# Chains of RWKV-7 in six phases that lanes go through in step, and TensorE's program in emission order

## The chip, the cores and the metric

The kernel runs on one core of one Trainium2 chip. The metric is the time of one execution on the device in microseconds (us); less is better. TensorE is written PE here, VectorE DVE, ScalarE ACT, GpSimd POOL and SyncE SP (it issues DMAs), as in the profile.

## The reference, cut to what matters

One layer of a diffusion backbone on 128 context tokens and 1024 latent tokens of 1024 channels, in float32. The hidden vector is projected once; half of the columns feed RWKV-7 (8 heads of 64, in two directions), half feed RG-LRU; both outputs are joined, projected and added to x under a gate; a gated feed-forward layer with a convolution follows. The change concerns the recurrence of RWKV-7 and what is computed beside it:

```python
def _wkv7_step(S, inp):
    r_t, w_t, kk_t, b_t, k_t, v_t = inp
    sa = jnp.einsum('dbhij,dbhj->dbhi', S, kk_t)
    S = S * w_t[..., None, :] - sa[..., :, None] * b_t[..., None, :] + v_t[..., :, None] * k_t[..., None, :]
    y = jnp.einsum('dbhij,dbhj->dbhi', S, r_t)
    return S, y

def block(x, cvec, s0, h0, grid, lp):
    mod = (jax.nn.silu(cvec) @ lp['w_mod'] + lp['b_mod'])[..., None, :]
    sh1, sc1, g1, sh2, sc2, g2 = jnp.split(mod, 6, axis=-1)
    h = rmsnorm(x, lp['ln1_g']) * (1.0 + sc1) + sh1
    proj = h @ lp['w_in']
    r, k, v, xw, xa, xg, xb, gb = jnp.split(proj, SPLITS, axis=-1)
    ya, s_fin = rwkv7_mix(r, k, v, xw, xa, xg, s0, ...)
    yb, h_fin = rglru_mix(xb, gb, h0, ...)
    x = x + g1 * (jnp.concatenate([ya, yb], axis=-1) @ lp['w_out'])
    h = rmsnorm(x, lp['ln2_g']) * (1.0 + sc2) + sh2
    u = dwconv(h @ lp['w_up'], lp['ffn_conv_w'], lp['ffn_conv_b'], CONV_F_LEFT, grid)
    ua, ub = jnp.split(u, 2, axis=-1)
    x = x + g2 * ((jax.nn.gelu(ua) * ub) @ lp['w_down'])
    return x, s_fin, h_fin
```

## The kernel before

The recurrence is computed in chunks of 64 tokens in each direction, two heads at a time. One visit to a chunk (both directions of a pair of heads) is a **hop**. A **lane** is a chain of hops that depend on each other through the state `S`; `chain` writes it as a Python generator. The program has two stretches of chains. In the first (437 to 737 us of the profiled execution) lanes a and b make 24 and 16 hops, beside the rest of the input projection and the RG-LRU branch (`rest_of_projection`: products `mm`, gate products `lg`, and long elementwise work and scans on DVE, ACT and POOL). In the second (737 to 960 us) lanes a, b, c and d make 8 hops each, beside the rest of the modulation (`mod_rest`, products `md` with `w_mod`, whose four quarters of the rows go to four column groups of the array), the RG-LRU half of the output projection (`wout_lru`, products `wo`) and `post` (the normalisation and gate of what the lanes leave, `po` on PE). The output projection's second half, and then the feed-forward layer (two thirds of the span), follow and are not touched.

On PE a hop is a row of small groups, each a few passes into one PSUM bank, which another engine empties. The names are the tiles' (the lane's letter last):

- `ya <- S, KR`: key and receptance rows times the state. Then `ya <- VS, G`, first halves; ACT and DVE (in the second stretch ACT alone, `use[1] = A`) copy the result to `R`.
- `ca <- R, TTp`: the inverse times `R`; copied to `VS` by the same engines.
- `ca <- VS, Kt`: the state's update, which DVE adds to `S`; then `ya <- VS, G`, second halves, copied to `o`.
- `prep` for the next hop, one step early: `pa <- kxa, BK` (DVE masks it into `G`; POOL scales `BK`), and `pa <- ident, BK` (transposes, which ACT copies to `Kt`). `fetch_keys` loads `BK` and, for a pair's second chunk, has ACT write the head blocks `kx`.

`chain` yields after the `R` copies, after the `VS` copies and at the hop's end. `run_all` takes a step from each generator in turn, in proportion to its count of steps, and so writes the program; a scheduler then orders each engine's instructions anew, by its own model of the times. Instructions of an engine run in that order on the chip. `deal` gives out the eight PSUM banks by name. In the first stretch each name of a lane has a bank of its own:

```python
deal(mm=(0, 1), lg=(0, 1), pa=(2,), ya=(3,), ca=(4,), yb=(5,), cb=(6,), pb=(7,))
```

and in the second all of `pa` to `pd`, `ca` to `cd` and `po` take banks 2 and 4 by turns, each name with a count of its own:

```python
two = (2, 4)
deal(ya=(3,), yb=(5,), yc=(0,), yd=(1,), pa=two, pb=two, pc=two, pd=two, ca=two[::-1], cb=two[::-1], cc=two[::-1],
     cd=two[::-1], md=(6,), wo=(7,), po=two)
run_all((lane_a, 98 - LA), (lane_b, 98 - LB), (lane_c, 26), (lane_d, 26), (posts(90), 90),
        (seq(mod_rest(16, 24), beside_all((mod_rest(24, 48), 30), (wout_lru(), 48))), FL))
```

The functions that the change touches, with the line numbers of the profile:

## Time and profile before

| | |
|---|---|
| median of 3 runs | 1852.57 us (1850.71 to 1853.16) |
| the profiled execution: time, span | 1849.17 us, 1847.5 us |
| PE busy, of the span | 1716.4 us, 93% |
| DVE, ACT, POOL busy | 69%, 47%, 39% |
| first stretch of chains | 437 to 737 us |
| second stretch of chains | 737 to 960 us |

Busy is the time in which an engine had an instruction under way; passes of PE overlap, so a group's end is not the next one's start. "Idle before" is the time an engine stood just ahead of an instruction, with what released it. The granted clock is the mean of TensorE's clock in a stretch, as a share of full speed (1.00 is 2.4 GHz, and 0.50 would be 1.2 GHz throughout).

### The profile page before, as it was taken

The numbers are of one execution on the slowest core, as the hardware profiler recorded it, in microseconds if no ns is written. First come the engines' busy times: TensorE is split into PE (matmuls) and PEld (weight loads), VectorE is DVE, ScalarE is ACT, GpSimd is POOL, SyncE is SP. The second block draws the span as 40 slices with busy tenths as digits, with TensorE's granted clock in tenths as the row PEclk, the third lists the DMA queues.
The fourth block names the chain that finished last, engine by engine and source line by source line (L and its number), as shares of the span: only waits on it lengthen the run. The fifth ranks groups of instructions, "written<-read, shape, count | busy, mean of one in ns | idle before, by whom it ended". The sixth has DMA issues, their size and how long they took to land.

```text
span 1847.5 us, 35759 instructions
## 1 busy us (share of the span) xinstructions
PE 1716.4 (93%) x13341; PEld 1442.9 (78%) x13341; DVE 1272.2 (69%) x2633; ACT 865.5 (47%) x1787; POOL 721.8 (39%) x742
## 2 busy tenths in 40 slices
PE   5998898888999989899988789999999998999996
PEld 4776676678777778456656689999999998888885
DVE  5458967797477664476788877676767667576764
ACT  6466655643666756333335844444444443121211
POOL 1022423322355344131121166666666663434340
PEclk8898979889999999899999899999999999999998
DMA  9254544443443434867775222222222225558571
GB/s 300 63 163 155 174 139 135 147 147 118 145 122 97 131 104 146 257 194 231 232 254 189 82 64 86 78 72 72 74 79 75 77 73 171 184 159 262 173 252 57
DMA packets 268428, 264.92 MB, mean 143 GB/s; under 512 B 21173, under 2 KB 218448, under 8 KB 268256
## 3 DMA queue, kind: packets, MB, share of 16 engines
q1 hardware_dynamic: 252496, 245.97, 42.1%
q10 hardware_dynamic: 15472, 16.54, 2.7%
q8 instruction: 105, 1.72, 0.4%
q14 instruction: 67, 0.55, 0.1%
q0 software_dynamic: 288, 0.14, 0.0%
HBM read 188.00 MB, written 74.58 MB: 142 GB/s over the span
## 4 chain that ended last, share of the span: by engine, by line
PE 66%; DVE 9%; ACT 3%; DMA 3%; issue 3%; POOL 3%; SPq 0%; ACTq 0%; POOLq 0%; DVEq 0%
PE acc L92 14%; PE x L92 7%; PE y L92 7%; PE z L92 7%; PE mm L92 7%; PE v L92 3%; PE wo L92 3%; PE ya L92 2%; PE lg L92 2%; PE md L92 2%; PE pa L92 2%; PE ca L92 1%; DVE X L501 1%; PE yb L92 1%; DVE gt L499 1%
## 5 line engine op out<-in xcount | busy, mean ns | idle before, releaser
L92 PE MATMUL mm<-h_hi,winp 128*128 128x384 f32 x1056 | 304.4, 358 | 4.9 <-DVE vr L808 3.2
L92 PEld LDWEIGHTS mm<-h_hi,winp 128*128 128x128 f32 x1056 | 198.7, 196 | 26.4 <-issue 14.9
L92 PE MATMUL mm<-h_lo,winp 128*128 128x384 f32 x528 | 187.7, 356 | 3.0 <-DVE h_lo L112 3.0
L112 POOL TENSOR_TENSOR wl<-raw,wh 128x512 fp32r<-128x512 f32 x110 | 155.1, 1412 | 69.7 <-ACT wh L106 69.4
L106 ACT ACTIVATE wh<-raw 128x512 fp32r<-128x512 f32 x110 | 69.5, 633 | 148.3 <-PE z L92 81.0
L92 PE MATMUL x<-f_hi,wh 128*128 128x256 f32 (+1 forms) x352 | 105.8, 301 | 8.9 <-ACT q L1652 5.3
L92 PEld LDWEIGHTS mm<-h_lo,winp 128*128 128x128 f32 x528 | 103.7, 197 | 9.6 <-DVE h_lo L112 4.5
L1090 POOL TENSOR_TENSOR BK<-BK,pc 128x256 f32<-128x256 f32 x72 | 47.8, 664 | 150.5 <-PE pa L92 58.8
L92 PE MATMUL x<-f_lo,wh 128*128 128x256 f32 (+1 forms) x352 | 105.5, 300 | 0.2 <-DVE f_lo L112 0.2
L92 PE MATMUL y<-t_hi,wh 128*128 128x320 f32 (+1 forms) x352 | 104.9, 298 | 0.7 <-DVE q L1657 0.7
L92 PE MATMUL x<-f_hi,wl 128*128 128x256 f32 (+1 forms) x352 | 105.3, 299 | 0.0
L92 PE MATMUL y<-t_lo,wh 128*128 128x320 f32 (+1 forms) x352 | 104.7, 297 | 0.0
L92 PE MATMUL y<-t_hi,wl 128*128 128x320 f32 (+1 forms) x352 | 104.6, 297 | 0.0
L112 POOL TENSOR_TENSOR wl<-S,wh 128x512 fp32r<-128x512 f32 x44 | 57.7, 1311 | 105.6 <-ACT wh L106 105.6
L92 PE MATMUL acc<-f_hi 128*128 128x512 f32 x330 | 91.0, 397 | 3.2 <-ACT zf L1760 3.2
L108 POOL TENSOR_SCALAR t_hi<-raw 128x512 fp32r<-128x512 f32 x66 | 52.9, 804 | 81.6 <-PE acc L92 35.4
L1619 DVE SCALAR_TENSOR_TENSOR zf<-C,fcw,zf 128x567 f32<-128x567 f32 x66 | 63.5, 962 | 23.3 <-ACT zf L1617 23.3
L92 PEld LDWEIGHTS acc<-f_hi 128*128 128x128 f32 x330 | 63.1, 192 | 16.9 <-ACT zf L1760 3.7
L92 PEld LDWEIGHTS x<-f_hi,wh 128*128 128x128 f32 x352 | 67.9, 193 | 9.9 <-ACT q L1652 5.8
L112 DVE TENSOR_TENSOR t_hi<-raw,t_hi 128x512 fp32r<-128x512 f32 x66 | 48.1, 735 | 37.0 <-POOL t_hi L108 37.0
L1617 ACT ACTIVATE zf<-C,colB,fcw 128x576 f32<-128x576 f32 x66 | 57.3, 868 | 28.1 <-DVE C L1689 15.7
L600 POOL TENSOR_TENSOR kd<-kd,rk 128x512 f32<-128x512 f32 (+1 forms) x24 | 32.2, 1342 | 97.0 <-ACT kd L598 96.8
(516 smaller groups left out, 5211.1 us busy)
## 6 DMA issues: line engine op xcount, KB each, us to landing
raw<-in_w_down SPq DMA_DIRECT2D x132, 256.0 KB, 3.1
raw<-in_w_up SPq DMA_DIRECT2D x88, 256.0 KB, 3.0
wmod<-in_w_mod SPq DMA_DIRECT2D x68, 256.0 KB, 4.2
act_d<-zf SPq DMA_DIRECT2D x44, 288.0 KB, 2.2
src<-act_d SPq DMA_DIRECT2D x66, 192.0 KB, 3.8
win<-in_w_in SPq DMA_DIRECT2D x44, 256.0 KB, 3.9
KR<-kb_d SPq DMA_DIRECT2D x36, 256.0 KB, 3.2
VS<-v_d SPq DMA_DIRECT2D x36, 256.0 KB, 3.2
```

Source lines behind the costliest of these rows:

```text
L92: PE.matmul(out, lhsT, rhs, start=start, stop=stop, skip_group_check=True)
L106: A.activation(hi, src, AF.Copy)
L108: eng.tensor_scalar(hi, src, 1.0, 0.0, op0=OP.mult, op1=OP.add)
L112: eng.tensor_tensor(lo, src, hi.bitcast(F32), op=OP.subtract)
L499: V.tensor_tensor(tv, X[:, q + 1:32, q:q + 1].to_broadcast([128, m, q]), X[:, q:q + 1, 0:q].to_broadcast([128, m, q]), op=OP.mult)
L501: V.tensor_tensor(X[:, q + 1:32, 0:q], X[:, q + 1:32, 0:q], tv, op=OP.add)
L600: G.tensor_tensor(self.kd, self.kd, self.k, op=OP.mult)
L1090: G.tensor_tensor(bk, bk, pc_f[q.f][:, :, x:x + 1].to_broadcast([128, 2, 128]), op=OP.mult)
L1617: A.activation(u, src, AF.Identity, scale=fcw[:, 1, m:m + 1], bias=colb("ffn_conv_b", m))
L1619: V.scalar_tensor_tensor(dv[:, :, 1:64], sv[:, :, 0:63], fcw[:, 0, m:m + 1], dv[:, :, 1:64], op0=OP.mult, op1=OP.add)
```

## The change

`chain` has six phases for each hop, A to F, with a yield behind each: A is `S` times `KR` (in the second stretch also the first step of `prep`, `L.ahead`), B the first halves of `G` and the copies to `R`, C the inverse and the copies to `VS`, D the first step of `prep` (first stretch), E the update of the state, the second halves and the copies to `o`, F the second step of `prep`, the head blocks (split from `fetch_keys`) and the spill. `phase` takes the same phase of two lanes one behind the other. The lanes' order, and where other work stands between the phases, are written out in two loops, and `Feed` hands the other work out in given shares. `tc.manual_schedule` keeps PE's instructions in the order in which they are written; the other engines are scheduled as before. `mod_rest` asks for six `w_mod` tiles ahead and writes the four products of four tiles one behind the other; `bg_p` takes a step of two posts at a time; the first step of `wout_lru`, which loads and rounds the weights, comes ahead of the second loop.

```diff
@@
+    class Together(Background):
+        def step(self):
+            for g in self.q[:2]:
+                try:
+                    next(g)
+                except StopIteration:
+                    self.q.remove(g)
+            return bool(self.q)
+
+    bg_a, bg_l, bg_i, bg_k = [Background() for _ in range(4)]
+    bg_p = Together()
@@
-        if n_ == 1:
-            for e in range(2):
-                A.activation(L.kx[half(e), :, :, e, :], q.KR[half(e)], AF.Copy)
+    def head_blocks(L, q):
+        for e in range(2):
+            A.activation(L.kx[half(e), :, :, e, :], q.KR[half(e)], AF.Copy)
@@
                 mm(py[:, 128 * d:128 * d + 128], q.KR[:, d, n_], Sc[:, d, :], d == 0, False)
+            if L.ahead:
+                next(ahead, None)
+            yield
...
                 copy(use[d], q.V[sh, n_, d, :], ps[sh, 0:128])
-            next(ahead, None)
+            yield
+            if not L.ahead:
+                next(ahead, None)
             yield
...
+            yield
             for _ in ahead:
                 pass
-            yield
+            if n_ == 0 and i + 1 < len(pairs):
+                head_blocks(L, qs[i + 1])
...
                     spill(s_d[f], Sc.rearrange("p d c -> p (d c)"))
+            yield
@@
-    run_all((take(lane_a, LA), LA), (take(lane_b, LB), LB), (rest_of_projection(), 12 + (54 - 6 * len(EARLY)) * 4 // PK))
+    in_order = {mybir.EngineType.PE}
+    rest = Feed(rest_of_projection(), NREST, 24)
+    with tc.manual_schedule(engines=in_order):
+        phase((lane_a, lane_b))
+        phase((lane_a, lane_b))
+        for r in range(24):
+            lanes = (lane_a, lane_b) if r % 3 < 2 else (lane_a,)
+            for ph_ in "ABCDEF":
+                phase(lanes)
+                if ph_ in "DEF":
+                    rest.turn(1.0 / 3.0)
+        rest.finish()
@@
     def mod_rest(i0, i1):
+        todo = [(idx, k) for idx in range(i0, i1, 4) for k in range(8)]
+        raw = []
+        def ask(n):
+            for idx, k in todo[:n]:
+                raw.append(p2("wmod", bufs=6))
+                load(raw[-1], ins["w_mod"][0, 128 * k:128 * k + 128, 128 * idx:128 * idx + 512])
+            del todo[:n]
+        ask(6)
+        yield
         for idx in range(i0, i1, 4):
             ps = bank("md")
...
+            for k0 in (0, 4):
+                for i in range(4):
+                    mod_part(ps, slice(0, 512), k0 + i, raw[i], True)
+                del raw[:4]
+                yield
+                ask(4)
             row = p2("tm")
             A.activation(row, ps, AF.Copy)
+            yield
             mod_cols(idx, row, 4)
             yield
@@
-    run_all((lane_a, 98 - LA), (lane_b, 98 - LB), (lane_c, 26), (lane_d, 26), (posts(90), 90),
-            (seq(mod_rest(16, 24), beside_all((mod_rest(24, 48), 30), (wout_lru(), 48))), FL))
+    for L in (la, lb, lc_, ld_):
+        L.ahead = True
+    of_lru = wout_lru()
+    next(of_lru)
+    late = Feed(seq(mod_rest(16, 24), beside_all((mod_rest(24, 48), 24), (of_lru, 48))), FL, 17)
+    with tc.manual_schedule(engines=in_order):
+        ab, cd = (lane_a, lane_b), (lane_c, lane_d)
+        phase(cd)
+        for h in range(17):
+            x, y = (ab, cd) if h % 2 == 0 else (cd, ab)
+            late.turn(1.0 / 3.0)
+            bg_p.step()
+            if h > 1:
+                phase(x)
+            elif h == 1:
+                phase(cd)
+            late.turn(1.0 / 3.0)
+            bg_p.step()
+            if h < 16:
+                phase(x)
+            late.turn(1.0 / 3.0)
+            if h > 0:
+                phase(y)
+            bg_p.step()
+            if h < 16:
+                phase(x)
+            if h > 0:
+                phase(y)
+                phase(y)
+        phase(cd)
+        late.finish()
```

The rows below are instructions in the order in which an engine runs them: line, operation, tile written, tiles read, shape of the tile or the stream, and how many follow each other. Line 1094 of the kernel before is line 1109 of the changed one.

**PE in the middle of the first stretch.** Before, at one of lane a's hops:

```order
L1094 MATMUL pa<-ident,BK 128x128 x2
L92 MATMUL pb<-kxb,BK 128x256
L92 MATMUL ca<-VS,Kt 64x64 x4
L92 MATMUL ya<-VS,G 64x64 x3
L92 MATMUL cb<-R,TTp 64x64
L92 MATMUL lg<-xl,gwh 128x384
L92 MATMUL cb<-R,TTp 64x64 x3
L92 MATMUL lg<-xh,gwl 128x384
```

Now, at a round of both lanes:

```order
L92 MATMUL ya<-S1a,KR 128x128 x2
L92 MATMUL yb<-S1b,KR 128x128 x2
L92 MATMUL ya<-VS,G 64x64 x4
L92 MATMUL yb<-VS,G 64x64 x4
L92 MATMUL ca<-R,TTp 64x64 x4
L92 MATMUL cb<-R,TTp 64x64 x4
L92 MATMUL pa<-kxa,BK 128x256 x2
L92 MATMUL pb<-kxb,BK 128x256 x2
L92 MATMUL mm<-h_hi,winp 128x384
```

A group is no longer cut by work of others; the copies to `R` have no other work of PE between `G` and the inverse; and twelve products of the projection stand behind D, E and F each. At the start of the stretch the last inverses of the stage before, both lanes' first `prep` and first hops now stand with no product of the projection or of the gates between them, and the first such product comes behind both lanes' first phase E.

**PE at the start of the second stretch**, behind the last row of the first (the transpose of `lru_fin`). Before:

```order
L997 MATMUL lg<-ident,lru_fin 8x128
L92 MATMUL pc<-kxc,BK 128x256 x2
L1094 MATMUL pc<-ident,BK 128x128 x2
L92 MATMUL pd<-kxd,BK 128x256 x2
L1094 MATMUL pd<-ident,BK 128x128 x2
L92 MATMUL pa<-kxa,BK 128x256
L92 MATMUL ca<-R,TTp 64x64 x2
L92 MATMUL md<-wmod,silx 32x512 x2
```

Now:

```order
L1009 MATMUL lg<-ident,lru_fin 8x128
L92 MATMUL md<-wmod,silx 32x512 x8
L92 MATMUL ya<-S0a,KR 128x128 x2
L92 MATMUL pa<-kxa,BK 128x256 x2
L92 MATMUL yb<-S0b,KR 128x128 x2
L92 MATMUL pb<-kxb,BK 128x256 x2
L92 MATMUL ya<-VS,G 64x64 x4
```

and on SP, which issues the loads of `w_out` (`wm`) and of `w_mod` (`wmod`), behind the store of `lru_o`, now:

```order
L1012 DMA out<-lru_o 8x128
L1330 DMA lnx<-in_rw_lnx_g 128x512
L1330 DMA lnx<-in_rw_lnx_b 128x512
L1444 DMA wm<-in_w_out 128x512 x3
L1396 DMA wmod<-in_w_mod 128x512 x2
L1444 DMA wm<-in_w_out 128x512 x3
L1396 DMA wmod<-in_w_mod 128x512 x2
L1444 DMA wm<-in_w_out 128x512 x2
L1396 DMA wmod<-in_w_mod 128x512 x2
```

The eight `md` products, which need eight `wmod` tiles, have moved ahead of all of the lanes' work, and all eight loads of `w_out` ahead of the sixth to eighth `wmod`; the second three `wm` wait until the first are rounded, since there are three buffers. Before, SP issued four `wmod` in a row here and `w_out` later.

**PE in the middle of the second stretch**, now (in brackets, the engines whose work a row waits for):

```order
L92 MATMUL ca<-R,TTp 64x64 [waits Activation_49]
L92 MATMUL ca<-R,TTp 64x64 x3
L92 MATMUL cb<-R,TTp 64x64 [waits PE_49,Activation_49]
L92 MATMUL cb<-R,TTp 64x64 x3
L1379 MATMUL po<-ident,osq 128x128 [waits DVE_49]
L1379 MATMUL po<-ident,osq 128x128
L1379 MATMUL po<-ident,osq 128x128 [waits PE_49,Activation_49]
L1379 MATMUL po<-ident,osq 128x128
```

The partner's group follows at once in the same bank, so that `cb` waits for ACT's copies of `ca` to `VS`. In the same way stand `ca <- VS, Kt` ahead of `cb <- VS, Kt` (DVE's additions), `pa <- kxa` ahead of `pb <- kxb` (DVE's `G`), `pa <- ident` ahead of `pb <- ident` (ACT's `Kt`), and the same rows of c and d.

## Rows read from the trace of the kernel before

**Rows 1.** Windows: us, busy us and passes of PE, PEld, DVE, ACT, POOL; clock; DMA.

```profile
437.00:737.00 300.00, 284.54 (x2684) 230.77 (x2684) 183.20 (x377) 191.22 (x387) 131.81 (x143) 0.97 0.40 124
737.00:960.00 223.00, 209.14 (x1688) 136.08 (x1688) 152.16 (x441) 80.99 (x226) 45.35 (x67) 0.96 0.73 232
...
740.00:765.00 25.00, 19.86 (x103) 9.42 (x104) 10.33 (x32) 6.88 (x17) 3.70 (x6) 0.74 0.69 212
570.00:600.00 30.00, 27.71 (x271) 21.38 (x267) 24.94 (x46) 17.09 (x34) 18.95 (x15) 1.00 0.31 87
```

**Rows 2.** What PE waited for, 437 to 737 us: us in total, times, longest.

```profile
PE ca L92 <- DVE R L1077: 5.7, 3, 4.9
```

**Rows 3.** The same view, 737 to 960 us.

```profile
PE pc L92 <- DMA BK<-kb_d: 6.8, 1, 6.8
```

**Rows 4.** Groups of PE's instructions by line, 437 to 476 us.

```profile
L92 PE MATMUL mm<-h_hi,winp 128*128 128x384 f32 x43 | 12.1, 359 | 0.0
L92 PE MATMUL mm<-h_lo,winp 128*128 128x384 f32 x22 | 8.3, 377 | 0.0
L92 PE MATMUL lg<-xh,gwh 128*128 128x384 f32 x10 | 4.2, 422 | 2.4 <-ACT kxa L1065 1.9 <-ACT th L880 0.2
```

**Rows 5.** Timeline of PE in the same stretch: start, us, instruction, count.

```profile
450.04 0.34 PE L92 MATMUL mm<-h_lo,winp 128*128 128x384 f32 x1
...
450.56 0.33 PE L92 MATMUL mm<-h_lo,winp 128*128 128x384 f32 x1
```

**Rows 6.** Timeline of PE from 603 us.

```profile
603.81 0.32 PE L92 MATMUL ca<-R,TTp 64*64 64x64 f32 x2
...
604.91 0.44 PE L92 MATMUL ca<-R,TTp 64*64 64x64 f32 x6
```

**Rows 7.** Timeline of all engines from 773 us.

```profile
773.94 0.69 DVE L1087 TENSOR_TENSOR G<-pd,mask 128x512 f32<-128x512 f32 x1 [1.32 <-PE pd L92]
...
775.39 0.38 ACT L1095 ACTIVATE Kt<-pb 128x256 f32<-128x256 f32 x1
...
775.57 0.45 PE L92 MATMUL yc<-VS,G 64*64 64x64 f32 x8
...
776.45 0.57 ACT L1075 ACTIVATE R<-yc 64x128 f32<-64x128 f32 x2
...
776.77 0.74 PE L92 MATMUL cc<-R,TTp 64*64 64x64 f32 x8 [0.76 <-ACT R L1075]
...
777.64 1.41 SPq L1381 DMA_DIRECT2D wm<-in_w_out  x3
777.69 0.57 ACT L1075 ACTIVATE VS<-cc 64x128 f32<-64x128 f32 x2
778.02 0.34 PE L92 MATMUL cc<-VS,Kt 128*64 128x64 f32 x4 [0.51 <-ACT VS L1075]
```

**Rows 8.** Timeline of PE at 836 us.

```profile
836.03 1.07 PE L92 MATMUL md<-wmod,silx 128*32 128x512 f32 x8
```

**Rows 9.** Groups of PE's instructions, 737 to 960 us.

```profile
L92 PE MATMUL md<-wmod,silx 128*32 128x512 f32 x128 | 35.4, 617 | 0.0
```

**Rows 10.** Groups of DVE's instructions, 437 to 737 us.

```profile
L911 DVE TENSOR_TENSOR_SCAN th<-th,colA,a 128x1024 f32<-128x1024 f32 x8 | 20.2, 2527 | 0.0
L1077 DVE COPY R<-ya 64x128 f32<-64x128 f32 x24 | 6.9, 288 | 10.9 <-ACT R L1075 10.6
...
L1185 DVE TENSOR_TENSOR S1a<-ca,S1a 64x128 f32<-64x128 f32 x24 | 6.9, 288 | 6.1 <-PE ca L92 5.7
```

**Rows 11.** Groups of ACT's instructions, 437 to 737 us.

```profile
L880 ACT ACTIVATE th<-lg,gab 128x384 f32<-128x384 f32 x24 | 13.9, 581 | 6.2 <-PE lg L92 6.0
```

**Rows 12.** Timeline of SP, 734 to 750 us.

```profile
738.45 0.48 SPq L1272 DMA_DIRECT2D lnx<-in_rw_lnx_b  x1
...
744.36 1.89 SPq L1341 DMA_DIRECT2D wmod<-in_w_mod  x4
```

**Rows 13.** The page's DMA issues: count, KB, us to landing.

```profile
wmod<-in_w_mod SPq DMA_DIRECT2D x68, 256.0 KB, 4.2
```

More of the change, by code (lines that the diff above doesn't have):

```diff
@@ L22 @@
 SPAN = ((0, 384), (384, 768), (768, 1152))
-LA = 74
+NREST = 70
 NT4, NAB4, NAG, NP, NL4, NC2 = 2, 4, 10, 1, 6, 6
@@ L963, in finish @@
                 self.step()
-    bg_a, bg_l, bg_i, bg_k, bg_p = [Background() for _ in range(5)]
+    class Together(Background):
[8 more added lines that the diff above has]
+    bg_p = Together()
     def beside(gens, *rates):
@@ L1032, in __init__ @@
             self.pool, self.k, self.py, self.pc, self.pp = pool, k, "y" + k, "c" + k, "p" + k
+            self.ahead = False
         def ring(self, name, n, bufs=2):
@@ L1111, in chain @@
         fetch_keys(L, qs[0], 1)
-        yield from prep(L, qs[0], 0)
+        yield
+        head_blocks(L, qs[0])
+        for _ in prep(L, qs[0], 0):
+            pass
+        yield
         Sc = None
@@ L1227, in tile_hybrid_step @@
     E, LATE = range(1, 5), range(5, NT)
-    lane_a = chain(Lane(rp, "a"), [(0, p) for p in E] + [(f, 0) for f in range(4)] + [(2, p) for p in range(1, NT)])
-    lane_b = chain(Lane(rp, "b"), [(1, p) for p in E] + [(3, p) for p in range(1, NT)])
+    la, lb = Lane(rp, "a"), Lane(rp, "b")
+    lane_a = chain(la, [(0, p) for p in E] + [(f, 0) for f in range(4)] + [(2, p) for p in range(1, NT)])
+    lane_b = chain(lb, [(1, p) for p in E] + [(3, p) for p in range(1, NT)])
     PB = 2
@@ L1238, in tile_hybrid_step @@
     XP = 2
-    FL = 88
+    FL = 83
     XC = 3
@@ L1243, in tile_hybrid_step, with __init__, turn, finish @@
     LB = 52
-    def take(g, n):
-        for _ in range(n):
-            next(g)
-            yield
-    run_all((take(lane_a, LA), LA), (take(lane_b, LB), LB), (rest_of_projection(), 12 + (54 - 6 * len(EARLY)) * 4 // PK))
+    class Feed:
+        def __init__(self, g, n, turns):
+            self.g, self.share, self.credit = g, n / turns, 0.0
+        def turn(self, part=1.0):
+            self.credit += self.share * part
+            while self.credit >= 1.0:
+                self.credit -= 1.0
+                next(self.g, None)
+        def finish(self):
+            for _ in self.g:
+                pass
+    def phase(lanes):
+        for g in lanes:
+            next(g, None)
+    in_order = {mybir.EngineType.PE}
[10 more added lines that the diff above has]
+        rest.finish()
     ph.close()
@@ L1263, in of_output @@
         return pw if name in ("woh", "wol", "yb", "ybh", "ybl") else p3
-    lane_c, lane_d = [chain(Lane(lcd, k, pq), [(f, p) for p in LATE]) for f, k in ((0, "c"), (1, "d"))]
+    lc_, ld_ = [Lane(lcd, k, pq) for k in "cd"]
+    lane_c, lane_d = [chain(L, [(f, p) for p in LATE]) for f, L in ((0, lc_), (1, ld_))]
     def p2(name, dt=F32, bufs=2):
@@ L1327, in post @@
         yield
-    def posts(n):
-        for _ in range(n):
-            bg_p.step()
-            yield
     def mod_rest(i0, i1):
+        todo = [(idx, k) for idx in range(i0, i1, 4) for k in range(8)]
[7 more added lines that the diff above has]
+        yield
         for idx in range(i0, i1, 4):
             ps = bank("md")
-            raw = []
-            for k in range(8):
-                raw.append(p2("wmod", bufs=6))
-                load(raw[k], ins["w_mod"][0, 128 * k:128 * k + 128, 128 * idx:128 * idx + 512])
-                if k % 2:
-                    yield
-                if k % 4 == 3:
-                    for i in range(k - 3, k + 1):
-                        mod_part(ps, slice(0, 512), i, raw[i], True)
+            for k0 in (0, 4):
+                for i in range(4):
+                    mod_part(ps, slice(0, 512), k0 + i, raw[i], True)
+                del raw[:4]
+                yield
+                ask(4)
             row = p2("tm")
             A.activation(row, ps, AF.Copy)
+            yield
             mod_cols(idx, row, 4)
```

## The prediction

> **What bounds the kernel now.** I read the windows by stage first. PE is busy in 284.5 of the 300 us of the first stretch of chains and in 209.1 of the 223 us of the second [rows 1], at granted clocks of 0.97 and 0.96; no other engine comes near. So PE's program is the bound in both, and an edit to its order can win in two ways only: fewer busy microseconds for the same passes, or less of the 15.5 and 13.9 us of idleness. Next, what PE waits for: in the first stretch the worst is `ca` on DVE's copy to `R`, 5.7 us in three waits [rows 2]; in the second one DMA at the start, 6.8 us [rows 3]. The waits inside the chains hardly show. The scheduler cuts groups and fills the gaps with other work, and pays for that in passes: an inverse in two pieces takes 0.32 + 0.44 us busy [rows 6], a group of eight passes of that size left whole 0.45 [rows 7], so a cut costs about 0.31. What a chain looks like without filling stands at 775 us, where lane c is alone: 0.76 us from `G` to the inverse behind ACT's two copies (0.57), 0.51 from there to the update [rows 7].
>
> The change trades cuts for waits: groups stay whole, but PE runs what is written, and waits where before it did something else.
>
> **First stretch, part by part.**
> *Cuts removed.* The order shows up to three groups of a hop cut (inverse, second halves, `prep`); 40 hops x 3 x 0.31 = 37 us at most, 12 at one cut each. Since whole products of the projection lie in one piece too, I take 30 off.
> *The start.* Until the first hop of lane a was done at about 476 us, PE had 65 `mm` and some 30 `lg` passes to put between the inverses, which wait on each other, and the first `prep` [rows 4]. Three such passes take 0.52 us from start to start [rows 5], 0.17 each: 95 x 0.17 = 16 us. In the changed order none stands there, and the inverses and first hops wait on the same chain of engines as before, so these 16 us come behind. Bounds: 0, if that chain gets shorter by as much, which no row suggests, and 16. I take 16.
> *New waits.* A pair of lanes gives 0.76 less the partner's `G` (0.45) for the first, and about as much for the second, whose copies queue: 0.6 us a round, 16 rounds; a round of lane a alone 0.76, 8 rounds: 16 us. Four gate products in a row go through two banks, each emptied by ACT in 0.58 us [rows 11] against 0.52 for three passes: 15 such groups x 0.5 = 7 us. A copy that DVE takes up behind a scan of 2.5 us, of which there are eight [rows 10], makes PE wait 1.25 us on average, where before it had other work: about 9. Together 32. Idleness of before, about 10 us outside the start (15.5 less some 5), goes: net 22.
> The first stretch: -30 + 16 + 22 = **+8**. Bounds: -15 (all of 37 saved, half of the waits) and +32 (12 saved, waits 28 net).
>
> **Second stretch.**
> *Busy time.* `md` has 128 passes in 35.4 us [rows 9]; eight passes together in four column groups take 1.07 [rows 8]. 16 such groups make 17.1, so 18 us go. 32 hops, 0.8 of a cut each, give 8 more. 209 - 18 - 8 = 183.
> *The start.* The eight `md` passes stand first, the lanes behind them. SP has stored `lru_o` and asked for `lnx` by 738.9 [rows 12]; three `wm` take 1.4 us to issue [rows 7], two `wmod` 0.9 (half of 1.89, [rows 12]); the next three `wm` wait until the first have landed (at 4.2 us, as `wmod` [rows 13]) and been rounded (like `G`, some 0.7 us for each of two engines), so until about 746; then two more `wmod`, landing at about 752.5; the last four behind two more `wm` and behind buffers that the first four `md` give back, so at about 757. From the end of the first stretch, 737, that is 20 us without lanes' work. Before, 6.8 us were idle there [rows 3], which is the lower bound; 25 the upper.
> *The partner's bank.* In each round the second lane's groups wait until the first one's bank is emptied. Inverse: from its start to the update behind the copies 1.25 us, less the 0.45 of its own passes: 0.75 [rows 7]. Update: two additions of DVE at 0.29 [rows 10] and 0.2 of latency, less the second halves between (0.4): 0.4. `prep`: `G` 0.69 [rows 7] and 0.2, less the partner's `KR` (0.5): 0.4. Transposes: `Kt` 0.38 [rows 7] and some 0.1: 0.5. The second `po` behind its partner's eviction: 0.45. Sum 2.5 us, in 16 rounds 40 us. Bounds: 16 (1.0 a round: the inverse's wait has no work of PE between, and a little of the rest) and 64 (4.0: the copies queue behind ACT's other work).
> *One bank for `wo`.* Where two products of 12 passes follow each other the second waits for DVE, 0.7 as for `G`: 5 us in all; 0 to 10.
> The second stretch: 183 + 20 + 40 + 5 = 248 against 223: **+25** (bounds -17 and +59).
>
> The posts in twos move DVE's and ACT's work, not its amount; DVE is busy in 152 of 223 us [rows 1], and the posts are nobody's input until the stretch ends. The head blocks move a phase later on ACT, which is busy in 81 of 223; nothing is priced for either. If ACT were full, each copy (0.27) behind a head block would cost PE up to 0.6.
>
> **The clock.** From 570 to 600 us PE is idle in 2.3 of 30 us, in small pieces, and granted 1.00; from 740 to 765, after one idle piece of 6.8 us, 0.74 [rows 1, 3]. Waits of under a microsecond are thus priced at full clock, and only the start of the second stretch is slow.
>
> The Trainium skill (TensorE: Matmul & The Clock Gate, "A second HAM failure mode: psum-queue depth-cycling") tells of a kernel whose small idle pieces between groups, as PSUM banks went round, were enough to send the clock back and forth between its two levels. That speaks against this change; rival 4 is what it would do here. The windows above do not bear it out so far, since 570 to 600 us keeps its clock.
>
> **Sum.** 8 + 25 = +33 on the profiled execution's 1849.2 us (span 1847.5 and 1.7 around it): 1882. The median of the runs stands 3.4 above the profiled one: **1885 us**.
>
> **Rivals.**
> 1. *Faster: the waits are mostly covered.* I priced 32 + 40 = 72 us of new waits from the bare chain. Before, 72 hops went by with waits under 30 us in all [rows 1]; if whole groups let ACT and DVE empty a bank while the partner's passes run, and `Kt`, `G` and the copies come at a fifth of my price, 57 us go: 1828. Against it: the order makes the partner wait for the very bank. The change gains once the waits sum to under 39 us.
> 2. *The start of the second stretch is cheap*: `wmod` lands in time, 7 us idle as before: 1872. For it: a load takes 4.2 us only; against it, the `w_out` loads ahead on SP.
> 3. *Long operations in the first stretch*: ACT's and DVE's long work beside the gates holds up both lanes in step, twice as much as I took and the copies of both: +20, 1905.
> 4. *The clock falls* in the second stretch because of its many waits, to a mean of 0.85 from 0.96: 188 us of passes x (0.96 / 0.85 - 1) = +24, 1909.
> 5. *Nothing to measure*: gains and waits cancel, within 0.2% (3.7 us, about what a measurement of this kernel tells from no change): 1852.
>
> **Chances.** Forecast 0.41 (its own range 1870 to 1902), rival 1 0.31, rival 2 0.10, rival 3 0.08, rival 4 0.06, rival 5 0.04. Of rival 1, 0.01 lies within 0.2%. So slower 0.65, same 0.05, faster 0.30. The range reaches down into rival 1 and up past rivals 3 and 4: 1822 to 1915; outside lie the extremes of the bounds.
>
> **What would show it.** Right: PE's busy time in the second stretch near 185 us and idle pieces of 0.4 to 0.8 us on ACT's `VS`, DVE's `S` and ACT's `Kt` in each round; the stretch's first lane pass some 20 us behind the transpose of `lru_fin`; the first `mm` of the first stretch's loop at about 475 us; a granted clock near 0.95 but at that start. Wrong: waits in the chains of under 1 us a round (rival 1), `md` going at 745 us (rival 2), waits of more than 1.5 us on DVE's `R` behind scans (rival 3), a clock under 0.9 from 770 to 950 us (rival 4).

## The result, and the profile after

The changed kernel takes 1965.33 us (median of 4 runs, 1961.34 to 1969.33) against 1852.87 beside it (1850.71 to 1855.38): a ratio of 1.0599, 95% interval 1.0572 to 1.0626. It is slower, as forecast, but by 112 us and not by 33. The profiled span is 1961.8 us.

The first stretch ends, with the transpose of `lru_fin`, at 803 us where it was 737: +66, forecast +8. The second ends, with the last pass of `yd`, at 1070.4 us; its length is 267.6 us and was 219.8: +48, forecast +25. What follows takes as long as before. The windows by stage of the changed kernel (us, busy us and passes of PE, PEld, DVE, ACT, POOL; clock; DMA):

```profile
437.00:479.00 42.00, 24.06 (x364) 18.80 (x364) 12.82 (x35) 11.19 (x22) 10.86 (x17) 0.51 0.40 126
479.00:803.00 324.00, 265.81 (x2269) 229.34 (x2263) 164.65 (x336) 182.36 (x362) 116.14 (x124) 0.89 0.32 98
803.00:831.00 28.00, 10.45 (x18) 1.50 (x17) 14.61 (x41) 2.95 (x7) 6.08 (x9) 0.55 0.78 261
830.00:910.00 80.00, 62.22 (x519) 45.52 (x517) 34.84 (x97) 27.75 (x72) 14.04 (x22) 0.87 0.70 224
910.00:990.00 80.00, 65.30 (x557) 47.23 (x556) 49.12 (x151) 27.87 (x78) 12.89 (x20) 0.89 0.60 194
990.00:1071.00 81.00, 66.12 (x668) 48.43 (x666) 55.29 (x157) 24.27 (x79) 14.37 (x21) 1.00 0.47 154
803.00:1071.00 268.00, 203.08 (x1753) 142.64 (x1752) 153.87 (x444) 82.84 (x236) 47.38 (x72) 0.89 0.61 198
```

The two parts of the first stretch in the kernel before, to set beside the first two rows:

```profile
437.00:476.00 39.00, 35.17 (x435) 29.14 (x436) 20.46 (x49) 19.65 (x35) 12.35 (x21) 0.91 0.50 153
476.00:737.00 261.00, 249.37 (x2251) 201.64 (x2249) 162.74 (x328) 171.58 (x353) 119.46 (x123) 0.98 0.39 120
```

Length less busy is idleness. In the first stretch PE's idleness grew from 3.8 to 17.9 us at the start and from 11.6 to 58.2 us behind it: 61 of the 66 us. Busy time grew by 5 us, although the cuts are gone. In the second stretch idleness went from 13.9 [rows 1] to 64.9 us (+51) and busy time fell by 6 only, where 26 were forecast; these windows differ by 45 us and not by 48, since the one of before runs some 3 us past the stretch's end. The clock is the second thing to see: 0.97 and 0.96 [rows 1] became 0.85 (24.1 us at 0.51 and 265.8 at 0.89) and 0.89, and not at the second one's start alone.

What PE waited for in the first stretch from 479 us on (us in total, times, longest):

```profile
PE ca L92 <- ACT R L1090: 13.4, 14, 3.6
PE ca L92 <- DVE R L1092: 12.4, 8, 3.4
PE lg L92 <- ACT th L880: 6.5, 5, 2.8
PE mm L92 <- ACT th L880: 6.0, 4, 2.8
...
PE cb L92 <- DVE R L1092: 3.7, 2, 3.2
```

The inverse's wait on `R`, 5.7 us before [rows 2], is now 29.5. One such place, in the timeline of all engines:

```profile
604.46 2.34 DVE L911 TENSOR_TENSOR_SCAN th<-th,colA,a 128x1024 f32<-128x1024 f32 x1
604.64 0.27 ACT L1090 ACTIVATE R<-ya 64x128 f32<-64x128 f32 x1
...
606.72 0.58 DVE L835 SCALAR_TENSOR_TENSOR xc<-mm,colB,xc 128x378 f32<-128x378 f32 x1
607.34 0.29 DVE L1092 COPY R<-ya 64x128 f32<-64x128 f32 x1
...
607.68 0.44 PE L92 MATMUL ca<-R,TTp 64*64 64x64 f32 x6 [2.40 <-DVE R L1092]
```

ACT's half of `R` is there by 604.9; DVE is in a scan, takes another operation of 0.58 behind it, and copies its half 2.7 us later than ACT. PE stands, because the next row of its program is this inverse.

PE's waits in the second stretch, the rows of `w_mod`, of a state load and of the partner's bank:

```profile
PE md L92 <- DMA wmod<-in_w_mod: 17.6, 4, 10.3
PE cb L92 <- ACT VS L1090: 5.6, 8, 0.9
PE cd L92 <- ACT VS L1090: 5.4, 8, 0.8
PE yd L92 <- DMA S1d<-s_d: 5.0, 1, 5.0
PE pd L1109 <- ACT Kt L1110: 4.7, 7, 1.3
PE pb L1109 <- ACT Kt L1110: 4.6, 7, 0.8
PE pb L92 <- DVE G L1102: 3.7, 7, 1.6
PE pd L92 <- DVE G L1102: 3.1, 6, 0.9
PE cd L92 <- DVE S0c L1212: 2.3, 4, 0.6
PE cd L92 <- DVE S1c L1212: 1.9, 3, 0.6
...
PE cb L92 <- DVE S0a L1212: 1.7, 3, 0.6
PE cb L92 <- DVE S1a L1212: 1.7, 3, 0.6
```

Without the first and fourth these make 34.7 us, and with `po` (1.8) 36.5. One round in PE's timeline:

```profile
903.32 0.45 PE L92 MATMUL cc<-R,TTp 64*64 64x64 f32 x8
904.42 0.27 PE L92 MATMUL cd<-R,TTp 64*64 64x64 f32 x2 [0.65 <-ACT VS L1090]
...
906.37 0.45 PE L92 MATMUL cd<-VS,Kt 128*64 128x64 f32 x8 [0.62 <-DVE S1c L1212]
...
908.98 0.41 PE L1109 MATMUL pd<-ident,BK 128*128 128x128 f32 x2 [0.56 <-ACT Kt L1110]
```

The second lane's group waits each time for the engine that empties the first lane's.

At the stretch's start, PE:

```profile
802.79 0.27 PE L1009 MATMUL lg<-ident,lru_fin 128*8 128x128 f32 x1
813.40 2.48 PE L92 MATMUL md<-wmod,silx 128*32 128x512 f32 x4 [10.34 <-DMA wmod<-in_w_mod]
819.84 2.56 PE L92 MATMUL md<-wmod,silx 128*32 128x512 f32 x4 [3.96 <-DMA wmod<-in_w_mod]
824.73 2.79 PE L92 MATMUL md<-wmod,silx 128*32 128x512 f32 x4 [2.33 <-DMA wmod<-in_w_mod]
828.45 2.58 PE L92 MATMUL md<-wmod,silx 128*32 128x512 f32 x4 [0.93 <-DMA wmod<-in_w_mod]
830.96 1.22 PE L92 MATMUL ya<-S0a,KR 128*128 128x128 f32 x4
```

and the queue of SP that it waits for:

```profile
805.69 1.37 SPq L1444 DMA_DIRECT2D wm<-in_w_out  x3
807.11 1.21 SPq L1396 DMA_DIRECT2D wmod<-in_w_mod  x2
813.41 1.94 SPq L1444 DMA_DIRECT2D wm<-in_w_out  x3
815.40 1.48 SPq L1396 DMA_DIRECT2D wmod<-in_w_mod  x2
```

The `wmod` loads come in twos behind the `wm` loads, as forecast (all eight `wm` ahead of the fifth to eighth `wmod`, not of the sixth to eighth only), and the first lane pass starts 28 us behind the transpose.

### The profile page after: what moved, and what is told of

It is laid out like the page before. It is cut to its first block, busy times and chain, and to the rows that moved or that the text cites. A ratio compares the mean times of both kernels' runs of the same rounds, so it can differ in the third digit from the quotient of the medians.

```text
span 1961.8 us, 35815 instructions
## 1 busy us (share of the span) xinstructions
PE 1714.3 (87%) x13341; PEld 1464.1 (75%) x13341; DVE 1266.0 (65%) x2631; ACT 868.2 (44%) x1793; POOL 717.3 (37%) x742
## 4 chain that ended last, share of the span: by engine, by line
PE 44%; DVE 5%; ACT 2%; DMA 2%; issue 1%; POOL 1%; SPq 0%; DVEq 0%; ACTq 0%; POOLq 0%
PE acc L92 13%; PE x L92 7%; PE y L92 7%; PE z L92 7%; PE v L92 3%; PE wo L92 2%; PE mm L92 2%; PE md L92 1%; DMA v<-v_d 1%; POOL wl L112 1%; ACT VS L1090 0%; ACT xt L1579 0%; DMA wmod<-in_w_mod 0%; DVE G L1102 0%; DVE tm L1471 0%
## 5 line engine op out<-in xcount | busy, mean ns | idle before, releaser
L92 PE MATMUL mm<-h_hi,winp 128*128 128x384 f32 x1056 | 311.1, 364 | 11.3 <-ACT th L880 6.0
L92 PEld LDWEIGHTS mm<-h_hi,winp 128*128 128x128 f32 x1056 | 202.2, 199 | 34.7 <-issue 15.4
L92 PEld LDWEIGHTS x<-f_lo,wh 128*128 128x128 f32 x352 | 68.2, 194 | 0.5 <-DVE f_lo L112 0.4
```

Of the source, the lines that this page charges most:

```text
L92: PE.matmul(out, lhsT, rhs, start=start, stop=stop, skip_group_check=True)
```

## The experiments

Each is the changed kernel with one edit, unless it says otherwise; ratios are against the kernel before, on the same chip, with their 95% intervals. "End" is the end of a stretch as above. What comes "back" is a difference of medians from different chips; by the ratios it is 3 to 5 us less for e1 to e4 and e14, and within about 2 us of it for e5 to e8. Ends and windows are those of one trace for each kernel.

**Which stretch.** e1 and e2 let the scheduler order PE in one of the stretches, e14 in both, with the same emission.

```diff
-    with tc.manual_schedule(engines=in_order):
+    if True:
```

> The changed kernel with PE's order left to the scheduler in the first stretch; the second stretch keeps the written order. If it is the written order that costs (PE stands behind DVE's and ACT's copies with other work behind it), the first stretch returns from 366 us to about 300 to 310, and the time to about 1905. If it is the six phases and the shares in which other work is handed out, whoever orders PE, the first stretch stays above 345 us and the time above 1945.

> The changed kernel with PE's order left to the scheduler in the second stretch alone. If the written order costs there, the waits on the partner's bank go (some 36 us in the trace) and the lanes fill the 28 us at the start: the stretch goes from 270 us to about 225, the time to about 1920. If the start is a matter of SP's queue, the 28 us stay and the time is about 1935. If neither, above 1955.

> The changed kernel with PE's order left to the scheduler in both stretches. The two single releases gave 63 and 29 us; if they add, 1873, and the 20 us that are left belong to the six phases, the shares and the loads' order, not to the written order. If the first stretch's release already frees the second, about 1900.

e1: 1902.12 us, 1.0283 [1.0265, 1.0302]; first end 749.8. e2: 1936.21 us, 1.046 [1.0434, 1.0485]; second stretch 234.9 us. e14: 1869.00 us, 1.0097 [1.0065, 1.0129]. So PE's written order costs 63 us by e1 and 29 by e2, and the two about add up (96 together). Of e1's 63 only 53 lie in the first stretch; the second, which e1 leaves as it is, is 7 us shorter in its trace, 260.7 us (the last section comes back to this). The 16 us that remain come with the new emission itself; in e14's trace, which is 6 us above its median, the first stretch ends 14 us later than before (750.8) and the second is 13 us longer (233.2).

**The partner's bank.** e3 deals `pb`, `pd`, `cb` and `cd` in the other order, so that two lanes in step use different banks. PE's program stays the same row by row.

```diff
-pb=two, pc=two, pd=two, ... cb=two[::-1], ... cd=two[::-1]
+pb=two[::-1], pc=two, pd=two[::-1], ... cb=two, ... cd=two
```

> The changed kernel with banks 2 and 4 dealt the other way round to lanes b and d, so that partners never use the same bank one behind the other; PE's order is the same row by row. If the partner's bank is the price, the 36 us of waits on VS, Kt, G and S go, with some of the half clock that they bring: 1915 to 1930. If the waits only go to the next thing that the second lane needs, above 1950.

1931.33 us, 1.0443 [1.0416, 1.0471]: 34 us back. The second stretch in e3, from its first lane pass and as a whole:

```profile
832.00:1036.00 204.00, 175.09 (x1739) 132.19 (x1736) 136.68 (x400) 77.86 (x229) 41.67 (x63) 0.97 0.70 226
805.00:1036.00 231.00, 185.37 (x1758) 134.18 (x1757) 151.82 (x442) 81.44 (x238) 48.08 (x72) 0.92 0.71 229
```

The order is the same and the waits for the partner are gone, but others come up in their place (`po`, whose bank ACT empties to `VS`, 5.9 us, and `cc` on `VS`, 4.9): idleness falls by 19 us only, from 65 to 46. The other 18 are busy time, 203.1 to 185.4. Two things make it. The clock behind the start is 0.97 where 0.87 to 1.00 stood: busy time times what the clock lacks is 62.2 x 0.13 + 65.3 x 0.11 = 15 us from 830 to 990 us, and 175.1 x 0.03 = 5 in e3, so 10 are clock. Not all of that is shown to be the banks': in e1, e4 and e7, whose second stretch is the changed kernel's with the same waits, the clock behind the start is 0.95 or 0.96 as well, and the stretch takes 260 or 261 us; e3's takes 229.7. And a group ahead of a wait ends alone, while whole groups overlap:

```profile
882.42 0.45 PE L92 MATMUL ca<-VS,Kt 128*64 128x64 f32 x8 [0.80 <-ACT VS L1090]
882.71 0.40 PE L92 MATMUL ya<-VS,G 128*64 128x64 f32 x8
```

Here in e3 a group of 0.45 us is followed 0.29 us on. That lost overlap of 0.16 us, in the 56 waits of the ten rows of the partner's bank, is 9 us, an estimate. A wait can thus be paid three times: by its length, by the overlap, and by the clock.

**The R copies.** e4 gives the other work's first third behind B (between the copies and the inverse) and takes it from D. e7 has ACT make all copies, so that none stands behind a scan of DVE.

```diff
-                if ph_ in "DEF":
+                if ph_ in "BEF":
```
```diff
-    use = [A, V]
+    use = [A, A]
```

> The changed kernel with the first stretch's other work behind phases B, E and F in place of D, E and F, so that twelve passes (2.1 us) stand between the copies to R and the inverse. If PE's waits on R (29.5 us in the trace) are what the first stretch loses, and take the clock down with them, 30 to 45 us go: 1920 to 1935. If long operations of DVE and ACT are the cause, the same time is lost behind VS, now without cover but prep's 2 us: above 1950.

> The changed kernel with ACT making both copies to R and to VS in the first stretch, where DVE makes one of the two. If those copies wait in DVE's queue behind scans of 2.5 us and sums of 1.4 us, PE's waits on DVE's R (16 us) mostly go: about 1948. If ACT's own queue (1.3 us activations) holds them as long, or it is the chain of engines itself that takes the time, within 6 us of 1965, to either side.

e4: 1934.90 us, 1.0462 [1.044, 1.0484], 30 us back; first end 778.8. e7: 1936.01 us, 1.0446 [1.0419, 1.0473], 29 us back; first end 782.4. By the ends 24 and 20 us lie in the first stretch; 7 and 8 are the second's, which neither edits. In e4 the worst wait moves one phase on, to the update on `VS`, which now has no cover:

```profile
PE ca L92 <- DVE VS L1092: 13.1, 8, 4.2
PE ca L92 <- DVE R L1092: 9.8, 6, 4.2
```

Cover is worth more behind B than behind D, but wherever it lacks, DVE's late copies show. In e7 `ca` waits 11.0 us for `R` and PE's clock is 0.94 from 479 us to the end.

**The start of the first stretch.** e5 hands out three turns of other work around the first `prep` and hop.

```diff
+        rest.turn(1.1)
         phase((lane_a, lane_b))
+        rest.turn(1.1)
         phase((lane_a, lane_b))
+        rest.turn(1.0)
         for r in range(24):
```

> The changed kernel with three of the first stretch's 70 steps of other work (products of the projection and of the gates) written between the last inverses, the first prep and the first hops, where before the scheduler had put such work. If the empty start costs its idle time and, at 0.51 of full speed from 437 to 479 us, its clock, 15 to 22 us go: about 1945. If the start is bound by the loads and the inverses and the work has room later as well, under 6 us.

1921.07 us, 1.0355 [1.0327, 1.0383]: 44 us back, more than expected. A turn hands out 2.9 steps, so these are some nine of the 70, not three. PE is busy in 33.9 us from 437 to 479 (24.1 in the changed kernel) at 0.76; and the other work runs out some two rounds before the lanes, whose last rounds then stand beside the second stretch's start, where PE is busy in 20.9 of 28 us (10.5 in the changed kernel). Two starts were filled, so the sizes of the two are not told apart here.

**The start of the second stretch.** e6 asks for the first six `wmod` ahead of `w_out`.

```diff
+    mod_first = mod_rest(16, 24)
+    next(mod_first)
     next(of_lru)
```

> The changed kernel with the first six loads of w_mod issued ahead of those of w_out. If SP's order makes the 28 us at the start of the second stretch, the first md products go some 6 us earlier and the lanes behind them some 12 us: about 1952. If DMA itself or the buffers hold up md, under 5 us.

1953.11 us, 1.0534 [1.0505, 1.0563]: 12 us back, the number that was expected, but not for its reason. Counted from the transpose, the first `md` pass comes 1.8 us earlier (8.9 us for 10.6) and the first lane pass 4.5 (23.7 for 28.2), not 6 and 12. PE still waits 17.9 us for `wmod`, 8.6 for the first tiles and 7.4 for later ones. The rest lies behind the start, where e1, e4 and e7 are shorter too without an edit, so that the hit is in part luck.

**Together.** e8 makes e3 to e7 at once.

> All of it together: partners' banks opposite, other work behind B, E and F, the start filled, w_mod ahead of w_out, both copies on ACT. If the causes are separate, the savings add: 34 for the banks and 30 for phase B as measured, and 16, 12 and 10 as expected, 102 of the 113 us that the change lost: about 1862. If the copies on ACT and the cover behind B save the same waits, some 10 less: 1872. If something else still holds the chains, above 1885.

1870.94 us, 1.0101 [1.0071, 1.0131]: 94 of 112 us back. Singly the five gave 34, 30, 44, 12 and 29, in sum 149 (some 140 by the ratios); they share waits and covers.

**Work in the wait.** To see what the clock does when the wait is filled with useless passes, e9 adds a product behind `G` into the bank of `ya`, and e13 two products of constants into the bank of `pb`, which is free there, in each round (96 passes, 24 us in all at full clock).

```diff
+                if ph_ == "B":
+                    spare = bank("pb")
+                    for d in range(2):
+                        mm(spare[:, 256 * d:256 * d + 256], ident, mask[:, d].rearrange("p n t -> p (n t)"))
```

> The changed kernel with work added: in the first stretch each hop writes 256 unused columns of its y bank with one more product behind the first halves of G (0.5 us at full clock, 40 hops, 20 us in all), just where PE waits for the copies to R. If the waits also take the clock down (0.89 of full speed over the stretch), the product lies in idle time and brings some of the clock back: 1948 to 1960. If idle time alone counts, it changes nothing: 1961 to 1969. If the copies don't leave that much room, up to 20 us more: 1985.

> The changed kernel with work added between phases B and C of the first stretch: one round in each of 24 writes two products (1.0 us at full clock, 24 us in all) into the bank of pb, which is free there, so that unlike in the run with 256 columns of the y bank no copy to R waits for it. If PE's waits cost their idle time and the clock besides, the added work lies in the waits and gives clock back: 1945 to 1962. If the clock is no matter, it is hidden in the longer waits and shows in the others, 0 to 10 us: 1965 to 1975. If the waits end 1 us later with it (they are no idle time of PE alone), 1985.

e9: 1979.93 us, 1.0694 [1.0669, 1.0719]. It decides nothing, since the copies to `R` read that bank and so wait for the added product. e13: 1964.02 us, 1.061 [1.0575, 1.0644], the same as without. The window of e13, to set beside the second row of the changed kernel's:

```profile
479.00:803.00 324.00, 276.41 (x2338) 235.01 (x2334) 161.54 (x333) 181.75 (x358) 115.64 (x123) 0.92 0.31 97
```

In this trace the stretch ends at 806.4 us; in those of the changed kernel and of e2, e3 and e6, whose first stretch is the same, at 802.8 to 807.7. From 437 us to its end PE's busy time is 303.2 us, where the changed kernel has 289.7: it grew by 13.5 for passes worth 24, so all other passes took some 10 us less. The clock over the same windows, 0.88 for 0.85, makes 3% of 280, 8 us, of that. Idleness fell by 10 us only, so the waits alone don't hold the added work. Yet it cost nothing that can be told from the spread of the runs (the interval is some 6 us to either side).

**Four turns and three.** e10 has e3, e5 (with the share of later turns cut, so that the other work lasts), e6 and e7, turns behind B, D, E and F, and no `md` in the second stretch's first round; e11 the same with turns behind D, E and F.

```diff
-                if ph_ in "DEF":
-                    rest.turn(1.0 / 3.0)
+                if ph_ in "BDEF":
+                    rest.turn(1.0 / 4.0)
```

> As all five together, but with the other work of the first stretch behind B, D, E and F in quarters of a turn (so that neither R nor the first step of prep goes without cover), spread to the stretch's end, and with the first md products behind the lanes' first two phases of the second stretch. In the trace of all five, 16 us of PE's waits on G and 14 us of one wait for w_mod answer to these edits. If waits in PE's order are the cause, 20 to 30 us go from 1871: about 1846. If the lanes' chain of engines is itself the bound by now, above 1862.

> As the kernel with four turns, but with the other work behind D, E and F as in the changed kernel. With both copies on ACT, which queues less than DVE, the wait from G to the inverse is about 0.6 us a round of two lanes and 0.8 of one, some 16 us in 24 rounds, and the clock with it: 8 to 20 us above the kernel with four turns if cover behind B matters, equal within 5 if the work behind D was as good.

e10: 1891.59 us, 1.022 [1.0188, 1.0251], a miss. e11: 1894.68 us, 1.0235 [1.0206, 1.0264]. With the copies on ACT the cover behind B can't be told from cover behind D (3 us, within the intervals). Both are slower than e8. The traces suggest why, but no run tests it: in e8 the other work had run out early, and the lanes' last rounds (to 771 us) ran while the second stretch's first loads were under way, where that start stands bare here (PE is busy in 12.6 of the 30 us from 768, at 0.73, in e10).

**Before's first stretch with the second one mended.** In the diff below the first piece is in all four runs, the others from e15 on. e12 writes the first stretch by `run_all` and lets the scheduler order it, as before; in the second it keeps the written order with e3, e6 and no `md` in the first round. e15 also loads the states of c and d ahead of all else, and moves `w_mod` behind the lanes' loads and `w_out` to the second round; e17 holds all `md` back to the third round; e18 `w_out` too.

```diff
+    run_all((take(lane_a, 146), 146), (take(lane_b, 98), 98),
+            (rest_of_projection(), 12 + (54 - 6 * len(EARLY)) * 4 // PK))
...
+        if pairs[0][1] == 5:
+            Sc = next_state()
+            load(Sc.rearrange("p d c -> p (d c)"), s_d[pairs[0][0]])
...
         phase(cd)
+        next(mod_first)
```

> The first stretch handed to the scheduler and shared out by run_all as in the kernel before (with the six phases as steps), the second in the written order with partners' banks opposite, w_mod ahead of w_out and md behind the lanes' first phases. If what the written order saves in the second stretch is real (PE was busy 185 us there, against 209 before) and its waits are mended, the second stretch takes 205 to 212 us against 220, and the time is 1838 to 1846 with a first stretch as before. If six phases cost the scheduler's stretch the 13 us that they did with the order left free there: 1850 to 1858. If the second stretch isn't mended, above 1862.

> As the kernel with a free first and a mended second stretch (1861), with the start of the second stretch written for the lanes: the loads of c and d and their states (S1c, S1d) before those of w_mod, those of w_out one round later, the first md products in the second round. In the trace of that kernel PE stood 9 us for w_mod, 8.6 for S1c and some 10 for BK and POOL there, and took 180 us for what followed 790 us. If SP's order at the start is what is left of the loss, 15 to 25 us go: 1836 to 1846, below the kernel before. If md and wo then wait later instead, above 1855.

> As the kernel with the lanes first (1849), with all other work of the second stretch (md, wo) from the third round on in place of the second. In the trace of that kernel PE stood 9.2 us for w_mod behind the first two thirds of md, with the lanes behind. If the wait goes since the lanes' hops now cover the loads, 5 to 9 us go: 1840 to 1844. If md then waits for the same loads a round later, within 3 us of 1849; if the work is missed where the lanes wait for each other, slower by up to 5.

> As the kernel with md from the third round on, with the loads of w_out one round later too. If SP's queue still delays the lanes' and w_mod's loads by w_out, another 2 to 5 us go; if the rounded w_out now comes late for wo (or its rounding on POOL and DVE runs into the lanes), 2 to 8 us more than that kernel.

e12: 1861.31 us, 1.0044 [1.0029, 1.006], 15 us above the range that was expected of a mended stretch. The first stretch is as before (end 737.9); at the second's start the wait for `wmod` fell to 9.6 us, and `yc` waited 8.6 for the load of its state, which came behind fourteen `wmod` in SP's queue. e15: 1848.81 us, 0.998 [0.9961, 0.9998]. e17: 1844.79 us, 0.9965 [0.9947, 0.9982]: the lowest, 0.35% under the kernel before, but not told from e15 and e18 by the intervals. e18: 1846.33 us, 0.9971 [0.9957, 0.9985]. The windows of e17, first stretch, second, and the second behind its start:

```profile
437.00:735.00 298.00, 284.14 (x2657) 231.51 (x2656) 183.54 (x376) 196.74 (x392) 127.41 (x143) 0.97 0.41 125
735.00:959.00 224.00, 179.88 (x1724) 131.10 (x1722) 148.46 (x438) 79.11 (x228) 45.79 (x69) 0.93 0.75 236
...
790.00:959.00 169.00, 147.31 (x1468) 110.65 (x1468) 122.47 (x368) 64.12 (x191) 31.82 (x47) 0.98 0.73 230
```

The second stretch has 29 us less of busy time than before [rows 1] and 30 more of idleness, and so ends about where it did (958.7 us, before 956.4). The feed-forward layer's first pass starts 1.1 us earlier than before; the other 3 us of the 4 in the span come out of that layer, which no edit touched and which takes 813 to 819 us in the traces of all these kernels. So the traces don't show that the 0.35% is the order's.

**Everything mended, both orders written.** e16 has e15's second stretch and e10's first.

> PE in the written order in both stretches, with all that was mended: start filled, four turns a round spread to the end, both copies on ACT, partners' banks opposite, and the start of the second stretch as in the kernel with the lanes first. The kernel with four turns took 1892, of which 25 to 30 us were idle at the start of the second stretch (w_mod, S1c). If SP's order there is the cause, 1865 to 1875; if not, above 1885. Below 1853 only if the first stretch also loses its 30 us of waits, which nothing here takes away.

1879.43 us, 1.0153 [1.0118, 1.0187]. The first stretch ends at 760.2 (0.91 from 479 us on; 768.2 in e10, with the same first stretch), 24 us behind e15's: there the written order still costs, with every mend tried.

## Why the prediction was right in sign and wrong in size

By the windows, +66 in the first stretch and +45 in the second (48 by its ends) split as follows (clock: an estimate, busy time times what the granted clock lacks, after less before):

| | forecast | measured |
|---|---|---|
| first: cuts removed | -30 | -28 (what is left over of busy time, lost overlap in it) |
| first: start, idle | +16 | +14 |
| first: waits behind the start, net | +22 | +47 |
| first: clock | 0 | +33 (24.1 x 0.49 + 265.8 x 0.11, less 35.2 x 0.09 + 249.4 x 0.02) |
| second: idle in all | 65 for 14 | 65 for 14 |
| second: busy | 183 for 209 | 203 for 209 |

**Right.** The trade was as told: whole groups save passes' time, and waits cost more. The cuts, as what is left over, and the first start came out within 2 us, and the first `mm` of the loop starts at 479 us (forecast 475); of the start's 17.9 us of idleness 9.4 are one wait that the profile puts down to a load (`VS <- v_d`), which the prediction did not name. In the second stretch PE's own work is 185.4 us in e3, where 183 were worked out, and the idleness in sum is as forecast: the partner's bank 36.5 us (40), at the groups named, and the start 17.6 (20). That the sum agrees to 1 us is luck: the three priced terms came out 8 us lower, and 8 us of other waits, 5.0 of them for the load of `S1d`, had no price. The first lane pass came 28 us behind the transpose and not 20, since the `md` passes lie between the waits (16 passes in 10.4 us, at 0.55 of the clock; two groups of eight were priced at 2.1). Rival 1, that the waits are mostly covered, is out, and so is rival 2.

**"The clock": the step that failed.** Of the 80 us between 1885 and 1965 some 45 are clock, 33 in the first stretch and 12 in the second, and 25 the first stretch's waits (below). The prediction priced waits of under a microsecond "at full clock", from one stretch of 30 us with 2.3 us idle. In the second stretch the clock fell to 0.87 and 0.89 from 830 to 990 us; of the 20 us by which busy time exceeds the forecast, about 12 are clock (203.1 x 0.11 less 209.1 x 0.04 is 14; by the windows one by one, less) and 9 overlap that whole groups lose at a wait, which the sum did not have either. The 12 are one trace's: behind the start e1, e4 and e7 lost 7 to 9 us to the clock with the same waits, where the changed kernel lost 15. In the first stretch, where no rival had it, the clock is the largest part of the miss, and there the traces agree: 0.84 to 0.86 from 437 us to the end in the changed kernel, e2, e3 and e6, 0.97 before. It makes 33 us, 9 of them at the start, whose four `pa <- kxa` take 2.04 us (from 458.09 us) and 1.13 later (at 487.74). e4 agrees: with the same passes, 0.92 for 0.89 makes 3% of 260, 8 us, and its busy time is 9.7 less.

Rival 4 was this mechanism for the second stretch (+24, chance 0.06). The Trainium skill (TensorE: Matmul & The Clock Gate, "A second HAM failure mode: psum-queue depth-cycling") says that small idle pieces between groups, as banks go round, can make the clock swing between its levels. The trace agrees from 830 to 990 us (0.87 and 0.89); it does not from 990 to 1071, which keeps 1.00 with the same kinds of waits, and e3's 0.97 without the partner's waits is hardly above the 0.95 and 0.96 of e1, e4 and e7 with them.

**"New waits" in the first stretch: mis-sized.** The inverse's wait on `R` was priced 25 us (16 of the bare chain, 9 behind scans) and is 29.5; the gates' banks were priced 7 and took 12.5; the waits on `S`, `VS` and `xc`, some 11 us, had no price, nor had 5 us of smaller ones. In all 58 us of idleness stand behind the start where 32 of new waits were priced, and 11.6 of before's are gone where 10 were to go. The pieces of 2 to 3.6 us behind long operations are rival 3 in part; with the copies off DVE (e7) the stretch ended 20 us earlier, clock included.

**"The start" of the second.** The reason held (SP's order), and e12 shows what lies in it: `wmod` put first hands the wait to the next load in the queue. Only the orders of e15, e17 and e18, in which the loads of the waiting chain come first, came near before's length (225.8, 223.4 and 221.3 us against 219.8).

The measured price of the written order in the first stretch, 53 us by e1's end of it, was not all won back: against the scheduler's order before, 24 stay in e16. They were not taken apart.

## What to carry to other kernels

In an engine's fixed order, every wait of a chain wants other work, or a partner in another bank, written into it; before lanes go in step, check which bank each partner's group gets and which long operation can stand ahead of the copy. Price such a wait three times: by its length, by the overlap that its group loses, and by the clock that it may take from everything around it. Put the loads of the chain that will wait at the head of the queue, and moved work where PE would stand. Before a gain is put down to an edit, look at the stretches that the edit leaves alone: one of them moved by 8 us here.

## What the runs showed of the hardware

The clock does not follow the share of idleness. In the changed kernel it falls in short pieces between others at full speed; two windows of 10 us of one stretch of rounds:

```profile
850.00:860.00 10.00, 7.48 (x68) 6.64 (x70) 1.76 (x6) 3.42 (x10) 1.45 (x3) 0.52 0.95 315
870.00:880.00 10.00, 8.16 (x94) 5.45 (x93) 5.23 (x13) 2.83 (x10) 1.85 (x3) 1.00 0.80 257
```

The 80 us from 830 to 910, with 22% idle, have 0.87, and the 81 from 990, with 18% and waits of the same kinds, have 1.00; e3 keeps 0.97 with 14%, and the kernel before 1.00 with 8% from 570 to 600 us [rows 1]. In the first stretch fewer waits went with a higher clock: from 479 us on 0.92 with the same passes (e4) and with more of them (e13), against 0.88 to 0.90 in four traces of the changed kernel's order (its own, e2, e3 and e6).

In the second stretch the same program, with the same waits, had different clocks from one trace to the next. Behind the start, the changed kernel and e4, whose edit lies in the first stretch:

```profile
831.00:1070.40 239.40, 192.43 (x1737) 141.08 (x1736) 138.69 (x401) 79.68 (x229) 41.30 (x63) 0.92 0.59 191
807.00:1039.80 232.80, 186.28 (x1737) 135.18 (x1736) 138.51 (x399) 79.46 (x228) 40.49 (x63) 0.96 0.61 197
```

PE waits 47 us in both, 20% of either window is idle, and e4's is 6.6 us shorter. e9 and e13 are as the changed kernel (0.92), e1 and e7 as e4 (0.95). So such waits go with a lower clock, but they don't fix what it is; which pattern of idle pieces decides was not found.
